# Hybrid S5 / sparse-attention layer: bias products, splits, sums and last scalings placed elsewhere in the program

## The chip, the cores and the metric

The kernel runs on one core of one Trainium2 chip. The metric is the device time of one execution in microseconds; of several runs the median is given. The engines are PE (TensorE: matmuls and transposes), DVE (VectorE), ACT (ScalarE), POOL (GpSimd) and SP (SyncE, which here only issues DMAs; ACT issues some too).

## What is computed (the reference)

One decoder layer on x of 1024 x 1024 float32 (one sequence, 1024 tokens, model width 1024):

```python
h = rmsnorm(x, norm_attn_g)
[u | q | k_cmp v_cmp k_slc v_slc k_win v_win | gates | g_a g_b] = h @ W_in
y_a = up_a(glu(s5(u)))                 # S5: 32 groups of 16 channels, state 64
y_b = up_b(nsa(q, k/v per branch, gates, T5 bias))   # 8 heads, 2 kv heads, head size 64
x  += (sigmoid(g_a) * y_a + sigmoid(g_b) * y_b) @ W_out
x  += (silu(n @ W_gate) * (n @ W_up)) @ W_down,  n = rmsnorm(x)   # inner width 2816
out = rmsnorm(x)
```

## The kernel before, in words

All float32 products are made of three: each operand is split into a high part (`wh`, `shi`, `mhi`: a cast on ACT or POOL) and a low part (`wl`, `slo`, `mlo`: a subtraction on DVE), and PE does high x high, low x high, high x low. A weight unit goes through three stages: SP loads it (`wr`), one engine casts it, DVE subtracts. `W.ahead(s, n)` keeps `s` units split and `n` loaded ahead of the next use.

The program runs in stages, and each engine takes its instructions in the order in which the code is written.

- *Projection with S5 beside it* (to some 370 us). The projection's matmuls (L414 to L416, called projection matmuls here) are interleaved with a side program, one step of it for so many matmuls. The side program makes the S5 in eight batches `b`: `tables(b)` (seven POOL operations L850 to L856, then `sn`, `xt`, `cs` on ACT), ways in and out (DVE, POOL), then per batch transposes, the kernel `kz`, eight transfers `tz<-kz` on SP, and `c<-ut,tz` products. `bias()` made eight pairs of matmuls (32x384 results, L824), each followed by a copy `brs` on ACT and a DMA on ACT, as eight steps ahead of the first batch. DMAs of SP and ACT share eight counters in turn, and one waits for the one before it on its counter. Then come `compress` and `glu` (whose `z` is split in eight pieces).
- *Attention*, then `up_b`, the merge: the output projection (`units`, L1491 to L1493) for 8 token tiles tt in the order (0, 1, 4, 5), (0, 4), (1, 5), (2, 3, 6, 7), (2, 3), (6, 7); the add to x (L1497), squares (L1504), roots, `norm` (L1511), and the transposes (`turned` for tt < 4; `turn`: sums and three further matrices T0, T1, T2 for tt >= 4).
- *Feed-forward, up*: a Strassen-Winograd scheme with seven products per matrix and 22 matrices (`rest`). Beside each, `self.chain` carries the sums (ch) of an earlier matrix through: loads of `sd`, two pairs of additions on DVE, stores to `ss`.
- *Feed-forward, down* (`down`): seven products p in the order 1, 5, 6, 3, 7, 2, 4, each over f = 0 to 10 (`order`, 77 steps). Step n splits step n+2's operands (`sr` from `sd` or `ss`, a weight block), loads step n+4's, and makes 12 matmuls (four token tiles of three). `beside` hangs other work on a step: chain sums, loads of x1, adds of the products to x1, squares and the last scalings. The last three steps go token tile by token tile, with `finish` for tiles 4 to 7.

Of the kernel before, what the change touches and what calls it, by code (L numbers as in the profile page):

```python
# [16 lines left out]
P = 128  # L17
# [19 lines left out]
NEAR = 6  # L37
# [86 lines left out]
class Winograd:  # L124
# [200 lines left out]
    def rest(self, n, early):  # L325
# [21 lines left out]
        next(self.chain, None)  # L347
# [6 lines left out]
        GP.tensor_tensor(p5, u3, p5, op=OP.add)  # L354
# [9 lines left out]
        self.t2(n + 1)  # L364
        if not early:
# [21 lines left out]
class Kernel:  # L387
# [83 lines left out]
    def transposed(self, tags, xs, hi, lo, tt):  # L471

        nc = self.nc
        for h in range(2):
# [7 lines left out]
            nc.vector.tensor_tensor(lo[:, o[0], o[1]], v, hi[:, o[0], o[1]], op=OP.subtract)  # L482

# [334 lines left out]
    def bias(self, pool):  # L818

        nc = self.nc  # L820
        for h in range(8):
            b = self.bank("c")
            for i in range(2):
                nc.tensor.matmul(b[:, 0:384], self.rbb[i][:, h, :], self.ohr, start=i == 0, stop=i == 1)  # L824
            s = pool.tile([P, 384], F32, name="brs", tag="brs", bufs=2)
            nc.scalar.copy(s, b[:, 0:384])
            nc.scalar.dma_start(self.bd[h], s)
            yield
# [30 lines left out]
    def s5(self):  # L859
# [64 lines left out]
        yield from self.bias(self.bs)  # L924
        zb = None
        for b in range(NB):
# [56 lines left out]
            AC.activation(f(zb[:, h]), q, AF.Gelu_apprx_tanh)  # L983
            yield
# [8 lines left out]
    def compress(self, pool):  # L993
# [27 lines left out]
        for _ in range(6):  # L1021
# [58 lines left out]
    def glu(self, pool):  # L1080
        nc, V = self.nc, self.nc.vector
        parts = []
        for h in range(2):
            parts.append([pool.tile([P, 4, 512], FR, name=n, tag=n, bufs=2) for n in ("zh", "zl")])
            for k in range(4):
                self.split(*(x[:, k, :] for x in parts[h]), self.z[h][:, k, :], "act", "dve")
                yield
# [343 lines left out]
    def up_b(self, pool, m_):  # L1431
# [28 lines left out]
        for n in range(4):  # L1460
            w = self.W.next("w_up_nsa", 0, 4, 256 * n, 256, ("act", "dve"))
            ps = [(i, h, self.bank("a")) for i in range(2) for h in range(2)]
            for kk in range(0, 4, 2) if n == 0 else (None,):
                for i, h, b in ps:
# [5 lines left out]
                    if kk != 0:  # L1470
                        merged(b, 2 * n + i, h)

    def merge(self, pool, m, td, xd, ffn):
# [4 lines left out]
        x1, xns, sq, tmp, ps = {}, {}, {}, {}, {}  # L1478
# [46 lines left out]
        def turn(what, tt, tags="bc"):  # L1525

            at, c = slice(P * tt, P * tt + P), slice(P * (tt - 4), P * (tt - 4) + P)
            first = lambda i, j: m[i][:, 4 * j:4 * j + 4, c].bitcast(F32)
# [7 lines left out]
            if what == "sums":  # L1536
# [4 lines left out]
                V.tensor_tensor(t1, pb, first(0, 0), op=OP.subtract)  # L1541
                V.tensor_tensor(t1, t1, first(1, 0), op=OP.subtract)
# [12 lines left out]
            elif what == "T4":  # L1555
                V.tensor_tensor(t3, first(0, 1), t1, op=OP.subtract)
                V.tensor_tensor(t3, t3, first(1, 1), op=OP.add)
# [3 lines left out]
        def turned(tt):  # L1561
            self.transposed("bc", xns.pop(tt), m[0], m[1], tt)

        def units(tts, q, between):

            banks = [self.bank("a") for _ in tts]
            for u in range(4):
                w = unit(u, q)
                for i, tt in enumerate(tts):
# [5 lines left out]
                    if u == 3:  # L1575
                        add(tt, q, banks[i])
                        if q and tt < 6:
# [3 lines left out]
                for f, *a in between.get(u, ()):  # L1581
# [9 lines left out]
        units((1, 5), 1, {(0, "m"): [(norm, 0), (root, 4)], 0: [(norm, 4)],  # L1591
                          2: [(turned, 0)] + T(4, "transpose", "sums"), (3, "m"): T(4, "T1", "B22")})
        units((2, 3, 6, 7), 0, {(0, "m"): T(4, "T3") + [(norm, 1), (root, 5)] + T(4, "T2"),
                                0: [(norm, 5)] + T(4, "T4"), (1, "m"): [(load, 2), (load, 3)],
# [27 lines left out]
    def down(self, pool, sd, ss, xd):  # L1622
# [39 lines left out]
        def combine(n):  # L1662
            while len(rb) < min(n, len(order)):
# [3 lines left out]
                if p in (5, 6, 7, 4):  # L1667
# [27 lines left out]
        sums = {}  # L1695

        def square(x, ss):
            scr = dn.tile([P, D], F32, name="scr", tag="scr", bufs=1)
            AC.activation(scr[:, 0:512] if x.shape[1] == 512 else scr, x, AF.Square, accum_out=ss)

        def scaled(tt, c, r, eng):
            x = x1[tt][:, c]
            self.scaled(x, x, r, gf[:, c], eng)
            nc.sync.dma_start(self.out[P * tt:P * tt + P, c], x)
# [19 lines left out]
        def beside(p, f):  # L1724

            if p == 4 and f < 4:
                V.tensor_tensor(half(4 + f, 1), half(4 + f, 1), gf[:, 512:D], op=OP.mult)
            if p == 1 and f < 8:
                if f % 4 == 0:
# [260 lines left out]
```

## Time and profile before

| | |
|---|---|
| median of 3 runs | 1602.8 us (1601.49 to 1607.31) |
| the profiled execution | 1604.1 us, span 1602.3 us, mean granted PE clock 0.984 |
| PE busy | 1528.9 us, 95% of the span, 7796 matmuls |
| DVE, ACT, POOL busy | 1015.7, 659.4, 642.0 us |
| HBM read, written | 153.61 MB, 59.37 MB (133 GB/s over the span) |

The first line says what is to be explained, the second that the profiled execution stands 1.3 us above the median. PE is the engine with the most work; the others have slack on average, though not in every stage. The page's slices show PE below 80% in two of 40 only.

### The profile page before, as it was taken

The page shows a single profiled execution, that of the slowest core. Times are in us where ns is not written, and L with a number is a line of the kernel's source. Part 1 is how long each engine was busy: PE and PEld are TensorE (multiplying, and loading weights), DVE is VectorE, ACT ScalarE, POOL GpSimd, SP SyncE. Part 2 cuts the span into 40 slices and gives each one's busy share as a digit, 9 for nine tenths or more (in the row PEclk, how much of TensorE's full clock was granted, in tenths as well). Part 3 has the DMA queues.
Part 4 walks back from the last instruction along what each step waited for, and adds up shares of the span by engine and source line. Part 5 has one row for each costly group of instructions (what it writes and reads, how often), then busy time and mean ns, then how long its engine had stood idle before and what let it go on. Part 6 is the DMA issues. An engine that isn't in the chain of part 4 may idle for free.

```text
span 1602.3 us, 22657 instructions
## 1 busy us (share of the span) xinstructions
PE 1528.9 (95%) x7796; PEld 1279.4 (80%) x7796; DVE 1015.7 (63%) x1916; ACT 659.4 (41%) x1354; POOL 642.0 (40%) x736
## 2 busy tenths in 40 slices
PE   8989999999999999999998989999999999799996
PEld 8867788888877899998777777888887877588884
DVE  7463786722335899998856665444456666486777
ACT  5221334411321698898126553333322223244444
POOL 1034767500012455555430128766777774000000
PEclk9999999999999999999999999999999999899998
DMA  7315343349247612100755522222235555875443
GB/s 222 107 63 168 112 139 98 81 117 266 84 151 231 184 30 66 43 28 16 223 181 168 197 79 79 79 86 86 79 112 182 194 177 204 285 234 173 128 133 125
DMA packets 184586, 216.59 MB, mean 135 GB/s; under 512 B 22810, under 2 KB 121526, under 8 KB 184471
## 3 DMA queue, kind: packets, MB, share of 16 engines
q1 hardware_dynamic: 175831, 199.93, 40.6%
q10 hardware_dynamic: 8640, 15.21, 2.6%
q8 instruction: 62, 1.02, 0.3%
q14 instruction: 53, 0.43, 0.1%
HBM read 153.61 MB, written 59.37 MB: 133 GB/s over the span
## 4 chain that ended last, share of the span: by engine, by line
PE 70%; DVE 10%; DMA 6%; ACT 5%; POOL 4%; issue 3%; SPq 1%; ACTq 0%; DVEq 0%; POOLq 0%
PE a L414 8%; PE a L416 7%; PE a L415 7%; PE O L1353 4%; PE a L220 4%; PE a L221 4%; PE a L222 4%; PE T L1335 3%; PE S L1237 3%; DVE wl L426 2%; DMA wr<-in_w_out 2%; ACT wh L423 2%; PE a L1721 2%; PE a L1722 2%; PE b L221 2%
## 5 line engine op out<-in xcount | busy, mean ns | idle before, releaser
L426 DVE TENSOR_TENSOR wl<-wr,wh 128x512 fp32r<-128x512 f32 (+1 forms) x142 | 160.0, 1139 | 140.8 <-ACT wh L423 96.1
L414 PE MATMUL a<-hhi,wh 128*128 128x512 f32 x448 | 183.5, 410 | 0.0
L416 PE MATMUL a<-hhi,wl 128*128 128x512 f32 x448 | 178.8, 399 | 1.5 <-DVE wl L426 1.5
L415 PE MATMUL a<-hlo,wh 128*128 128x512 f32 x448 | 178.5, 398 | 0.0
L1308 POOL TENSOR_SCALAR P<-P,sum,gates 128x640 f32<-128x640 f32 (+3 forms) x192 | 125.1, 667 | 115.6 <-DVE sum L1302 71.6
L220 PE MATMUL a<-mhi,wh 128*128 128x512 f32 (+1 forms) x360 | 139.1, 386 | 0.9 <-ACT p L235 0.3
L222 PE MATMUL a<-mhi,wl 128*128 128x512 f32 (+1 forms) x360 | 138.5, 385 | 1.0 <-DVE rstd L441 1.0
L221 PE MATMUL a<-mlo,wh 128*128 128x512 f32 (+1 forms) x360 | 138.4, 384 | 0.0
L423 ACT CAST wh<-wr 128x512 fp32r<-128x512 f32 (+1 forms) x110 | 78.0, 728 | 129.2 <-DMA wr<-in_w_out 40.9
L161 POOL TENSOR_SCALAR wr<-wr,gcol 128x256 f32<-128x256 f32 x176 | 94.3, 560 | 71.0 <-DMA wr<-in_w_ffn_up 68.1
L421 POOL TENSOR_SCALAR wh<-wr 128x1024 fp32r<-128x1024 f32 x32 | 33.7, 1052 | 205.6 <-PE a L415 116.6
L1337 DVE TENSOR_TENSOR PTl<-T,PTh 128x512 fp32r<-128x512 f32 (+3 forms) x200 | 104.2, 544 | 9.9 <-ACT PTh L1336 8.1
L414 PEld LDWEIGHTS a<-hhi,wh 128*128 128x128 f32 x448 | 85.4, 191 | 22.1 <-issue 4.1
L416 PEld LDWEIGHTS a<-hhi,wl 128*128 128x128 f32 x448 | 85.4, 191 | 22.1 <-DVE wl L426 1.9
L1288 ACT ACTIVATE P<-P,m 128x640 f32<-128x640 f32 (+7 forms) x128 | 95.8, 749 | 17.2 <-DVE m L1272 17.2
L415 PEld LDWEIGHTS a<-hlo,wh 128*128 128x128 f32 x448 | 85.6, 191 | 18.0
L423 ACT CAST shi<-sr 128x512 fp32r<-128x512 f32 x77 | 47.7, 620 | 122.5 <-issue 53.8
L1336 ACT CAST PTh<-T 128x512 fp32r<-128x512 f32 (+3 forms) x200 | 88.7, 476 | 20.8 <-PE T L1335 19.8
L426 DVE TENSOR_TENSOR wl<-S,wh 128x1024 fp32r<-128x1024 f32 x44 | 66.8, 1519 | 41.1 <-ACT wh L423 41.1
L1272 DVE CUSTOM_DVE_ANT_0 P<-S,B 128x640 f32<-128x640 f32 (+7 forms) x128 | 89.6, 700 | 2.8 <-PE T L1335 1.1
L1335 PE MATMUL T<-cst,P 128*128 128x128 f32 x592 | 87.2, 274 | 3.6 <-DVE PTl L1337 2.9
L426 DVE TENSOR_TENSOR slo<-sr,shi 128x512 fp32r<-128x512 f32 x77 | 54.5, 708 | 49.6 <-ACT shi L423 49.6
(445 smaller groups left out, 4069.6 us busy)
## 6 DMA issues: line engine op xcount, KB each, us to landing
wr<-in_w_in SPq DMA_DIRECT2D x28, 512.0 KB, 4.2
wr<-in_w_out SPq DMA_DIRECT2D x24, 512.0 KB, 5.1
wr<-in_w_ffn_gate SPq DMA_DIRECT2D x22, 512.0 KB, 4.0
wr<-in_w_ffn_up SPq DMA_DIRECT2D x22, 512.0 KB, 4.1
ch<-sd SPq DMA_DIRECT2D x44, 256.0 KB, 3.0
ss<-ch SPq DMA_DIRECT2D x44, 256.0 KB, 2.5
sr<-ss SPq DMA_DIRECT2D x44, 256.0 KB, 2.7
b<-in_w_ffn_down SPq DMA_DIRECT2D x38, 256.0 KB, 3.8
```

The lines of the kernel that those rows point to most:

```text
L220: mm(o, wh[:, k], bh[:, k, c], start=first and k == 0, stop=False, skip_group_check=True)
L221: mm(o, wh[:, k], bl[:, k, c], start=False, stop=False, skip_group_check=True)
L222: mm(o, wl[:, k], bh[:, k, c], start=False, stop=k == 3, skip_group_check=True)
L414: mm(ps, a, c, start=start and k == 0, stop=False, skip_group_check=True)
L415: mm(ps, a, d, start=False, stop=False, skip_group_check=True)
L416: mm(ps, b, c, start=False, stop=stop and k == nk - 1, skip_group_check=True)
L423: nc.scalar.copy(hi, src)
L426: (nc.gpsimd if lo_eng == "pool" else nc.vector).tensor_tensor(lo, src, hi, op=OP.subtract)
L1288: AC.activation(p[:, 0:nk], p[:, 0:nk], AF.Exp, bias=m[:, 0:1], scale=-1.0, accum_out=sm(0))
L1308: sc = lambda x, y, z: GP.tensor_scalar(x, x, a[:, y:y + 1], gate(z), op0=OP.mult, op1=OP.mult)
L1335: T.transpose(t[:, x, :], p[:, c:c + P], self.ident)
L1337: V.tensor_tensor(ol, t[:, 0:len(cc), :], oh, op=OP.subtract)
```

## The change

- `bias(pool, h)` makes one pair and is called once in each batch, after that batch's gelu; the side program has four empty steps where it had eight with a pair each.
- `compress` starts one step later; `glu` takes two steps per split instead of one.
- `up_b` calls `W.ahead(2, 4)` after its first row of the last unit.
- In `merge`, the squares and roots of tiles 4 and 5 and the T1/B22 splits come later; `turned` also copies the transposed banks to `raw` (two ACT copies per tile), and the sums subtract `raw` in one DVE operation where they subtracted high and low halves in two.
- In `rest`, the chain's step comes after `t2(n + 1)`; the last matrix's products and one add go from POOL to DVE.
- In `down`, the chains of the last two matrices move from (1, 0) to (1, 7) to other steps; sums of squares and the weight's `combine` are spread over earlier steps; the last scalings are done half by half, half 0 on DVE with its store on SP, half 1 on ACT with its store on ACT, with roots for 4, 2 and 2 tiles together.

```diff
@@ out(): last matrix
-            K.nc.gpsimd.tensor_tensor(t, t, self.gates.pop((j, i, h)), op=OP.mult)
+            eng = K.nc.vector if n + 1 == len(self.mats) else K.nc.gpsimd
+            eng.tensor_tensor(t, t, self.gates.pop((j, i, h)), op=OP.mult)
@@ rest()
         self.t1(n + 1)
-        next(self.chain, None)
...
         self.t2(n + 1)
+        next(self.chain, None)
@@ s5(), ahead of the batches, and in each
-        yield from self.bias(self.bs)
+        for _ in range(4):
+            yield
...
             AC.activation(f(zb[:, h]), q, AF.Gelu_apprx_tanh)
+            self.bias(self.bs, b)
             yield
@@ up_b()
+                    if n == 3 and i == 0 and h == 1:
+                        self.W.ahead(2, 4)
@@ merge(): sums, turned
-                V.tensor_tensor(t1, pb, first(0, 0), op=OP.subtract)
-                V.tensor_tensor(t1, t1, first(1, 0), op=OP.subtract)
+                V.tensor_tensor(t1, pb, first(0), op=OP.subtract)
...
-            self.transposed("bc", xns.pop(tt), m[0], m[1], tt)
+            x = raw[tt] = xns.pop(tt)
+            for h, ps in enumerate(self.transposed("bc", x, m[0], m[1], tt)):
+                AC.copy(x[:, 512 * h:512 * h + 512], ps)
...
-        units((1, 5), 1, {(0, "m"): [(norm, 0), (root, 4)], 0: [(norm, 4)],
-                          2: [(turned, 0)] + T(4, "transpose", "sums"), (3, "m"): T(4, "T1", "B22")})
+        units((1, 5), 1, {(0, "m"): [(root, 0), (norm, 0), (square, 4), (root, 4)], 1: [(norm, 4)],
+                          2: [(turned, 0)] + T(4, "transpose", "sums")})
@@ down(): beside
-            if p == 1 and f < 8:
-                if f % 4 == 0:
-                    sums["chain"] = self.chain(pool, sd, ss, NF - 2 + f // 4)
+            at = {(1, 3): 0, (1, 10): 1}.get((p, f))
+            if at is not None:
+                sums["chain"] = self.chain(pool, sd, ss, NF - 2 + at)
+            if (p, f) in ((1, 3), (1, 6), (1, 7), (1, 8), (1, 10), (5, 2), (5, 3), (5, 4)):
                 next(sums["chain"])
...
+        def finish(tt, r):
+            rows = slice(P * tt, P * tt + P)
+            V.scalar_tensor_tensor(half(tt, 0), half(tt, 0), r, gf[:, 0:512], op0=OP.mult, op1=OP.mult)
+            nc.sync.dma_start(self.out[rows, 0:512], half(tt, 0))
+            AC.activation(half(tt, 1), half(tt, 1), AF.Copy, scale=r)
+            nc.scalar.dma_start(self.out[rows, 512:D], half(tt, 1))
...
         split(len(order))
+        r = roots(0, 0, 4)
+        for tt in range(4):
+            finish(tt, r[:, tt:tt + 1])
```

Three places show what the change moves. The first is ACT at the start of the S5 batches: `sn`, `xt`, `cs` are the tables' values, `uv` and `evf` copies of projection results, `cd` a store, `brs` and `bd` the bias copies and their stores, `wt` the first batch's transposes. Before:

```order
L880 ACTIVATE sn<-xt 128x512
L881 ACTIVATE xt<-xt 128x512
L882 ACTIVATE cs<-xt,cst 128x512
L638 COPY uv<-a 128x64 x8
L624 COPY evf<-a 128x512
L625 DMA cd<-evf 128x512
L826 COPY brs<-c 128x384
L827 DMA bd<-brs 128x384
L826 COPY brs<-c 128x384
L827 DMA bd<-brs 128x384
```

and now:

```order
L641 COPY uv<-a 128x64 x8
L627 COPY evf<-a 128x512
L628 DMA cd<-evf 128x512
L627 COPY evf<-a 128x512
L628 DMA cd<-evf 128x512
L936 COPY wt<-b 128x512
L627 COPY evf<-a 128x512
L628 DMA cd<-evf 128x512
L880 ACTIVATE sn<-xt 128x512
L881 ACTIVATE xt<-xt 128x512
L882 ACTIVATE cs<-xt,cst 128x512
L627 COPY evf<-a 128x512
```

The bias copies and stores have left this place, and the second tables' values (the second `sn`, `xt`, `cs`) stand ahead of a fourth `evf` copy and its store.

The second is DVE at the start of the down projection: `slo`, `wl` are the low halves of the steps' operands (`wr`, `near`, `b`: the weight blocks), `ch` the chain's sums. Before:

```order
L426 TENSOR_TENSOR slo<-sr,shi 128x512
L426 TENSOR_TENSOR wl<-wr,wh 128x512
L1612 TENSOR_TENSOR ch<-ch 128x512
L1613 TENSOR_TENSOR ch<-ch 128x512
L426 TENSOR_TENSOR slo<-sr,shi 128x512
L426 TENSOR_TENSOR wl<-wr,wh 128x512
L1615 TENSOR_TENSOR ch<-ch 128x512
L1616 TENSOR_TENSOR ch<-ch 128x512
L426 TENSOR_TENSOR slo<-sr,shi 128x512
L426 TENSOR_TENSOR wl<-near,wh 128x512
```

and now:

```order
L427 TENSOR_TENSOR slo<-sr,shi 128x512
L427 TENSOR_TENSOR wl<-near,wh 128x512
L427 TENSOR_TENSOR slo<-sr,shi 128x512
L427 TENSOR_TENSOR wl<-b_13000,wh 128x512
L427 TENSOR_TENSOR slo<-sr,shi 128x512
L427 TENSOR_TENSOR wl<-b_13029,wh 128x512
L1617 TENSOR_TENSOR ch<-ch 128x512
L1618 TENSOR_TENSOR ch<-ch 128x512
L427 TENSOR_TENSOR slo<-sr,shi 128x512
L427 TENSOR_TENSOR wl<-b_13053,wh 128x512
```

The sums of the chain of the last matrix but one stood behind the low halves of the third step and in front of those of the fourth; now five more steps' halves go ahead of them.

The third is ACT at the end, behind the last split: `rstd` are the roots, `x1f` the scaled halves, `out` their stores. Before, all of it for tiles 4 to 7:

```order
L1699 ACTIVATE scr,ssf_14394<-x1f 128x512
L1699 ACTIVATE scr,ssf_14423<-x1f 128x512
L440 ACTIVATE rstd<-ssf_14851,eps 128x1
L1758 ACTIVATE x1f<-x1f,rstd 128x512
L1759 DMA out<-x1f 128x512
L1699 ACTIVATE scr,ssf_14452<-x1f 128x512
L440 ACTIVATE rstd<-ssf_14875,eps 128x1
L1758 ACTIVATE x1f<-x1f,rstd 128x512
```

and now:

```order
L441 ACT_TABLE_LOAD
L441 ACTIVATE rstd<-sq_14801,eps 128x4
L1764 ACTIVATE x1f<-x1f,rstd 128x512
L1765 DMA out<-x1f 128x512
L1764 ACTIVATE x1f<-x1f,rstd 128x512
L1765 DMA out<-x1f 128x512
L1764 ACTIVATE x1f<-x1f,rstd 128x512
L1765 DMA out<-x1f 128x512
L1764 ACTIVATE x1f<-x1f,rstd 128x512
L1765 DMA out<-x1f 128x512
L1703 ACTIVATE scr,ssf_12937<-x1f 128x512 x2
L441 ACTIVATE rstd<-sq_14850,eps 128x2
```

The square-root table's load and four scalings with their stores (tiles 0 to 3) now stand in front of the squares of tiles 4 and 5.

## Rows read from the trace of the kernel before

**Rows 1.** The page, part 1: busy us of each engine, share of the span, instructions.
```profile
PE 1528.9 (95%) x7796; PEld 1279.4 (80%) x7796; DVE 1015.7 (63%) x1916; ACT 659.4 (41%) x1354; POOL 642.0 (40%) x736
```

**Rows 2.** PE's waits in the whole span: us in total, times, longest.
```profile
PE a L1721 <- DVE wl L426: 13.9, 4, 9.8
PE c L824 <- ACT brs L826: 6.6, 1, 6.6
PE b L222 <- DVE wl L426: 3.5, 6, 0.8
PE a L1491 <- DVE x L1497: 3.4, 2, 3.2
PE c L220 <- ACT T2h L423: 3.1, 1, 3.1
...
PE a L1491 <- ACT wh L423: 2.1, 2, 1.2
PE c L1045 <- DMA w<-in_cmp_w_k: 2.1, 1, 2.1
```

**Rows 3.** PE's timeline, 120 to 127 us: start, us, engine, line, operation, [idle before].
```profile
120.92 0.68 PE L824 MATMUL c<-ohr,rbh 32*128 32x384 f32 x1 [6.62 <-ACT brs L826]
...
122.87 0.63 PE L416 MATMUL a<-hhi,wl 128*128 128x512 f32 x1
...
126.71 0.63 PE L416 MATMUL a<-hhi,wl 128*128 128x512 f32 x1
```

**Rows 4.** ACT's timeline, 111 to 112 us.
```profile
111.07 0.63 ACT L880 ACTIVATE sn<-xt 128x512 f32<-128x512 f32 x1 [14.45 <-POOL xt L856]
```

**Rows 5.** DVE's timeline, 116 to 119 us.
```profile
116.43 1.88 DVE L426 TENSOR_TENSOR wl<-wr,wh 128x1024 fp32r<-128x1024 f32 x1
```

**Rows 6.** POOL's timeline, 148 to 160 us: first and last of seven.
```profile
148.34 1.04 POOL L850 TENSOR_TENSOR ta<-cst,rh 128x512 f32<-128x512 f32 x1
...
158.65 0.62 POOL L856 TENSOR_SCALAR xt<-xt 128x512 f32<-128x512 f32 x1
```

**Rows 7.** SP's queue, 147 to 155 us.
```profile
147.46 7.05 SPq L947 DMA_DIRECT2D tz<-kz  x8
```

**Rows 8.** PE's timeline, 161 to 162 us.
```profile
161.49 0.38 PE L977 MATMUL c<-ut,tz 128*128 128x128 f32 x2
```

**Rows 9.** PE's timeline, 1375 to 1381 us: first and thirteenth start.
```profile
1375.41 0.79 PE L1721 MATMUL a<-wl,shi 128*128 128x512 f32 x1 [9.76 <-DVE wl L426]
...
1380.64 0.40 PE L1721 MATMUL a<-wl,shi 128*128 128x512 f32 x1
```

**Rows 10.** DVE's timeline, 1372 to 1374 us.
```profile
1372.73 0.69 DVE L1612 TENSOR_TENSOR ch<-ch 128x512 f32<-128x512 f32 x1 [10.19 <-DMA ch<-sd]
```

**Rows 11.** SP's queue, 1362 to 1369 us.
```profile
1362.39 2.01 SPq L1619 DMA_DIRECT2D ss<-ch  x4
1366.83 1.75 SPq L1609 DMA_DIRECT2D ch<-sd  x4
```

**Rows 12.** PE's timeline, 1576 to 1583 us.
```profile
1576.85 0.39 PE L1722 MATMUL a<-wh,slo 128*128 128x512 f32 x1
1577.08 0.39 PE L1720 MATMUL a<-wh,shi 128*128 128x512 f32 x1
...
1582.44 0.80 PE L1721 MATMUL a<-wl,shi 128*128 128x512 f32 x1 [2.50 <-DVE wl L426]
```

**Rows 13.** ACT's timeline, 1565 to 1599 us (ACTq: its DMA issues).
```profile
1565.30 1.28 ACT L440 ACT_TABLE_LOAD   x1
1566.59 0.29 ACT L440 ACTIVATE rstd<-ssf,eps 128x1 f32<-128x1 f32 x1
...
1596.79 0.29 ACT L440 ACTIVATE rstd<-ssf,eps 128x1 f32<-128x1 f32 x1 [0.45 <-DVE rstd L441]
1597.76 0.72 ACT L1758 ACTIVATE x1f<-x1f,rstd 128x512 f32<-128x512 f32 x1 [0.68 <-DVE rstd L448]
1598.51 0.37 ACTq L1759 DMA_DIRECT2D out<-x1f  x1
```

More of the change, by code (lines that the diff above doesn't have):

```diff
@@ L36 @@
 NPOW = 9
-NEAR = 6
+NEAR, EARLY = 6, 9
 def run(gen, n=None):
@@ L353, in rest @@
         V.tensor_tensor(u3, u2, v, op=OP.add)
-        GP.tensor_tensor(p5, u3, p5, op=OP.add)
+        (V if last else GP).tensor_tensor(p5, u3, p5, op=OP.add)
         if last:
@@ L816, in bias_parts, with bias @@
         self.split(*self.rbb, rbb, "act", "dve")
[L818 to L828, printed above, removed]
+    def bias(self, pool, h):
+        nc, b = self.nc, self.bank("c")
+        for i in range(2):
+            nc.tensor.matmul(b[:, 0:384], self.rbb[i][:, h, :], self.ohr, start=i == 0, stop=i == 1)
+        s = pool.tile([P, 384], F32, name="brs", tag="brs", bufs=2)
+        nc.scalar.copy(s, b[:, 0:384])
+        nc.scalar.dma_start(self.bd[h], s)
     def exp(self, out, x, pool, name, n):
@@ L1020, in compress @@
         ws = [w1(j) for j in range(4)]
-        for _ in range(6):
+        for _ in range(7):
             yield
@@ L1694, in down @@
         Vs = [self.bank("bbcc"[i]) for i in range(4)]
-        sums = {}
+        sums = {i: dn.tile([P, 8], F32, name=f"ssf{i}") for i in range(2)}
         def square(x, ss):
[L1698 to L1704, printed above, removed]
+            AC.activation(dn.tile([P, 512], F32, name="scr", tag="scr", bufs=1), x, AF.Square, accum_out=ss)
         def add(tt, c, ps):
@@ L1735, in beside @@
                     x1_loads(range(at[0], at[0] + 4), at[1])
+            if p == 2 and f >= 6:
+                for i in range(2 * f - 12, min(2 * f - 10, EARLY)):
+                    V.tensor_tensor(slot[0, i], slot[2, i], slot[0, i], op=OP.subtract)
             tt = f - 2
@@ L1742, in beside, with roots @@
             if 0 <= tt < 4:
+                if p == 7:
+                    square(half(tt, 1), sums[0][:, 4 + tt:5 + tt])
+                    V.tensor_tensor(half(tt, 1), half(tt, 1), gf[:, 512:D], op=OP.mult)
                 if p == 2:
[L1744 to L1745 removed]
+                    square(half(4 + tt, 1), sums[1][:, 4 + tt:5 + tt])
+                    V.tensor_tensor(half(4 + tt, 1), half(4 + tt, 1), gf[:, 512:D], op=OP.mult)
                 if p == 4:
[L1747 to L1760 removed]
+                    square(half(tt, 0), sums[0][:, tt:tt + 1])
+        def roots(i, a, b):
+            sq = dn.tile([P, b - a], F32, name=f"sq{b - a}", tag=f"sq{b - a}", bufs=2)
+            V.tensor_tensor(sq, sums[i][:, a:b], sums[i][:, 4 + a:4 + b], op=OP.add)
+            return self.rstd(dn, sq)
+        def finish(tt, r):
[4 more added lines that the diff above has]
+            nc.scalar.dma_start(self.out[rows, 512:D], half(tt, 1))
         last = len(order) - 3
@@ L1775, in down @@
                 products(n, tt)
-            if tt < 3:
-                beside(*order[last + tt])
             add(4 + tt, 0, U[tt])
-            square(half(4 + tt, 0), sums[4 + tt][:, 0:1])
-            if tt:
-                finish(tt - 1)
-        finish(3)
+            square(half(4 + tt, 0), sums[1][:, tt:tt + 1])
+            if tt == 1:
+                r = roots(1, 0, 2)
+                finish(4, r[:, 0:1])
+            if tt == 2:
+                finish(5, r[:, 1:2])
+        r = roots(1, 2, 4)
+        for tt in range(2):
+            finish(6 + tt, r[:, tt:tt + 1])
         dn.release()
```

40 lines of the change are left out of this document (13 added, 27 removed).

## The prediction, on record before the run

> **What bounds the kernel now.** The page's busy shares come first: TensorE (PE) works 1528.9 of 1602.3 us, 95% [rows 1], so only some 73 us of idle time, and the stretches at the lower granted clock, can be won without taking matmuls away. The change takes none away: the PE list has the same number of rows in both programs. So I read the view that sums PE's waits by line and releaser, for which wait costs most [rows 2]. Three kinds stand out: one place in the down projection (L1721 for wl: 13.9 us in four waits, one of 9.8), one in the bias products (L824: 6.6), and small ones of 1.5 to 3.5 in compress, merge and the Winograd stage. Then I went to each place in the timelines, to see what the releaser itself had waited for.
>
> **The pitch of a matmul.** Two starts in a row at full clock are 0.23 us apart [rows 12]. After the bias wait nine matmuls take 126.71 - 122.87 = 3.84 us, 0.43 each [rows 3]: the lower of the two clock levels. A long wait thus costs more than itself.
>
> **1. Bias products, spread over the batches.** Before, the third pair starts at 120.92 after 6.62 us of waiting for a copy on ACT [rows 3]. ACT was in `sn<-xt`, before which ACT had idled 14.45 us for POOL's tables [rows 4]. The move takes this wait away and 9 x (0.43 - 0.23) = 1.8 us of low clock with it. But what is late next stands close: the matmuls behind it need a weight's low half, whose subtraction DVE starts at 116.43 and ends at 118.3 [rows 5]. PE, without the two pairs that ran before, would be there at about 113, and waits about 5 us again. Further on, the first S5 batch now comes 39 projection matmuls sooner. It needs `tz`, eight transfers that SP issued from 147.46 [rows 7]. In the changed program those stand, on the counter that they share with ACT's transfers, behind an ACT store that comes after `sn`, `xt`, `cs` of the second tables. POOL takes from 148.34 to 159.27 for these [rows 6]. If their start moves up with the weight unit ahead of them to about 128, they end at 137 to 139; the ACT work, the store and the eight transfers put `tz` at 147.5 to 151 (an estimate, middle 149.3). PE arrives at 143.5 to 147, so a new wait of 0 to 7 us. The same progress: before, `c<-ut,tz` starts at 161.49 [rows 8] with eight bias pairs and 39 matmuls more done; after, 149.3 + 39 x 0.23 + 8 pairs x 0.46 (two pitches each, an estimate) = 162.0, and the new waits bring the low clock back, another 1.8: 163.8. Term: **-2** (a loss of 2), from -6 to +4. The wait that goes is alone worth 6.6 + 1.8 = 8.4; `tz` takes it back. The copies (and their stores) beside the later batches stand under 39 matmuls per batch: nothing.
>
> **2. Compress and glu.** Compress starts one step later, about nine matmuls = 2.1 us, and PE's wait there for `w` is 2.1 [rows 2]: gain 0 to 2.1. Glu gets its splits two steps apart; DVE's low halves meet the weight's own there. I take **+1.5** for both (-1 to +3, a slip of four DVE pieces of 0.7 to one missed).
>
> **3. Splits ahead of the merge.** PE's first matmuls of the output projection wait for wh (two waits, 2.1 in all [rows 2]), then for its low half. ahead(2, 4) puts both on ACT and DVE some dozen matmuls sooner, before the square-root table load. **+2** (0 to +3: the wh wait in full and a us of low clock above, nothing if the weight's transfer is what is late).
>
> **4. Merge.** PE waits 3.2 us once for the add `x` (3.4 in two [rows 2]). On DVE the add stands behind a run of subtractions. Three of these, a T1 sum and two low halves, now stand behind it: 3 x 0.6 (0.69 each [rows 10], less the overlap of two in a row) = 1.8. The wait for T2h is 3.1 [rows 2]; the chain to it loses two DVE pieces a tile, of which I count the last tile's 1.2. Against it stand eight more copies on ACT, two a tile. They lie beside weight casts that PE waits for, and a copy of this size in front of a cast makes it up to 0.7 late (0.72 with a scale [rows 13]). 1.8 + 1.2 = **+3**; -2 (seven of the eight in front of a cast that PE waits for, 5, less the 3) to +6 (both waits gone).
>
> **5. The Winograd matrices.** One chain step is moved a sum later, and the last matrix's products go from POOL to DVE. Waits of the kind L222 for wl are 3.5 us in six [rows 2]; one or two may go. DVE takes three more pieces of 0.69 once. **+1** (-1 to +3).
>
> **6. Into the down projection.** The long wait is the clearest. DVE stands at `ch`, the chain of matrix 20, from its last low half to 1372.73, 10.19 us [rows 10], for a load that SP could only issue at 1366.83, after the store at 1362.39 [rows 11]. The low half that PE needs, ready to be made, is queued behind it, so PE waits 9.76 to 1375.41, then runs at the low clock: 12 matmuls to 1380.64 in 5.23 us [rows 9] where 12 x 0.23 = 2.8 would do, 2.4 lost. Together 12.2. The change moves this chain's load to (1,3), its sums to (1,6) and (1,7), three steps of 12 matmuls (2.8 us each) later than the load. So the low half is made where it is ready. What is late next: the SP queue. The same store and load still stand on it in order, and SP issues no operand load in the 4.4 us between [rows 11]. With loads four steps ahead (11 us), that gap and the chain's four transfers beside them, I take off one step's worth, 3: **+9** (4 to 13, the upper end with a smaller wait of the same line just before it).
>
> **7. The end.** The last token groups start at 1577.08, and PE waits 2.50 us at 1582.44 for a low half [rows 12]; on DVE the splits stood among wide scalings. Now the sums and combines are spread before, so 36 matmuls x 0.23 = 8.3 and up to a us of waiting end PE 9.2 after the start (call it 0). But the roots of tiles 0 to 3 and their scalings now stand behind the last split, on DVE and ACT, in front of the last tiles. ACT: the root is ready at about 4.0 with the table load of 1.28 in it (two splits of DVE before it, an estimate); four times a copy of 0.72 and an issue of 0.37, to 8.6 with hand-overs; two squares at the price of the copy to 10; a root (from 1596.34, where ACT began to wait for it, to the copy at 1597.76: 1.4) to 11.4; copy and issue 12.5; square and finish 14.4, square 15.1, root 16.5, two finishes to 18.8; and 3.8 from the last issue to the span's end (1602.3 - 1598.5) [rows 13]: 22.6. Before: 1602.3 - 1577.08 = 25.2. **+2.6** (1 to 5; a split of both halves over ACT and DVE helps only while ACT is not the longer).
>
> The table load has a rule of its own. Rows: the load starts at 1565.30, takes 1.28, and the root starts at 1566.59 [rows 13], 1.29 later. The Trainium skill, "ScalarE: Activation LUTs", section "What ACT_TABLE_LOAD costs", gives about 1.28 us for the load and about 1.38 more for a drain, 2.66 together. Here, where the load now lies on the end's path, the sum by it would be 1.4 less, 15.7; the trace shows no such drain, so the sum goes by the row.
>
> **The sum.** -2 + 1.5 + 2 + 3 + 1 + 9 + 2.6 = 17.1 us. The profiled execution took 1604.1 (a span of 1602.3 and 1.8 around it), 1.3 over the median; 1604.1 - 17.1 = 1587.0, and against the median 1585.7. I predict **1586 us**, 1.0% faster.
>
> **Rivals.**
> A. The forecast: 1580 to 1591. The large term is a wait whose cause (one load ahead of splits in a queue) is in plain sight. Chance 0.60.
> B. The transition wait only moves: SP's loads, behind the store's 4.4 us, come late for the first steps, and 9 turns to 3. Sum 11, 1592. For it: SP issued no operand load for more than a step there [rows 11]. Against it: sr is four steps ahead. 0.16.
> C. Nothing much: transition 3, the bias term -4 (`tz` at 151), and ACT's copies eat the merge's gain (0). Sum -4 + 1.5 + 2 + 0 + 1 + 3 + 2.6 = 6: 1597, within 0.5% (8 us, about what can be told from no change). 0.17.
> D. Slower: the batches, 39 matmuls earlier, each wait for POOL's tables. A table takes 10.9 us [rows 6]. If each of eight batches stood 4 us for it, that is 32 in place of the 2 I took: 1603 - 19 + 32 = 1616. It decides from (19 + 8)/8 = 3.4 us a batch. Against it: only the first batch comes sooner against its tables; all later ones keep their distance in the matmul list. 0.07.
>
> So faster by over 0.5% is 0.76 (A, B), no difference 0.17, slower 0.07. The range is 1576 to 1598: A with the bias products and the transition at their good ends (+6 and +4 more), B, and most of C.
>
> **What the trace will show.** Right: no wait of the L1721 line (renumbered) over 3 us between 1355 and 1385; DVE's `ch` sums beside splits with no 10 us idle; the last store issued within 19 us of the last groups' start; a wait near 113 to 118 and one for `tz` in the place of the bias wait. Wrong: a wait of 5 us or more for `sr` in the first ten steps of the down projection (B); waits for `tz` or the tables in most batches (D); ACT ahead of a cast in the merge (C).

## The result, and the profile after

The changed kernel takes 1595.5 us (median of 5 runs, 1592.2 to 1597.1) against 1604.0 for the kernel before in the same session (5 runs, 1601.5 to 1607.3): the ratio is 0.994, with a 95% interval of 0.9918 to 0.9962. It is faster by 8.5 us, within the range on record, but the gain is half of the 17.1 us forecast. The profiled execution has a span of 1595.3 us, 7.0 below the 1602.3 of before. PE's busy time is the same to 0.1% [rows 1].

The page after, part 1, busy us by engine:

```profile
PE 1527.5 (96%) x7796; PEld 1282.1 (80%) x7796; DVE 1003.0 (63%) x1898; ACT 664.8 (42%) x1368; POOL 639.6 (40%) x732
```

To see where the time went I took the start times of matmuls that both programs have, and compared the stretches between them. The stretches, in us of the two profiled executions (gain positive):

| stretch of PE | before | after | gain | forecast |
|---|---|---|---|---|
| start of the program to the first projection matmul | 48.5 | 49.8 | -1.3 | 0 |
| to the first attention score (terms 1, 2) | 461.5 | 466.1 | -4.6 | -0.5 |
| to the last attention product | 248.3 | 248.0 | +0.2 | 0 |
| up_b, then output projection to the first Winograd product (terms 3, 4) | 166.0 | 167.1 | -1.1 | +5 |
| Winograd matrices, to the down projection (term 5) | 431.4 | 430.8 | +0.6 | +1 |
| first 11 steps of the down projection (term 6) | 45.0 | 34.1 | +10.9 | +9 |
| next 55 steps | 154.0 | 154.8 | -0.8 | 0 |
| last product to the span's end (term 7) | 47.8 | 44.7 | +3.1 | +2.6 |

The gains sum to 7.0, the difference of the spans. The last part of the program won what was forecast and a little more; the first half lost what was to be won there.

PE's waits in the whole span after, the costliest lines (us in total, times, longest), against [rows 2]:

```profile
PE c L978 <- DMA tz<-kz: 8.1, 1, 8.1
PE a L220 <- ACT p L235: 6.3, 5, 1.5
PE a L1496 <- DVE x L1502: 5.6, 3, 2.3
PE a L415 <- POOL m L906: 4.6, 1, 4.6
...
PE c L1047 <- DMA w<-in_cmp_w_k: 1.9, 1, 1.9
...
PE a L1720 <- DVE wl L427: 1.7, 2, 1.4
```

The 13.9 us in the down projection are down to 1.7, and the bias wait of 6.6 is gone. In their place stand three waits that were not on the list before (`tz`, ACT's `p`, POOL's `m`), and the waits for x have grown from 3.4 to 5.6. The first and the fourth line are the S5's start. PE's timeline after, 118 to 153 us, answering to [rows 3, 8]:

```profile
118.37 0.54 PE L415 MATMUL a<-hhi,wh 128*128 128x512 f32 x1 [4.59 <-POOL m L906]
...
152.59 0.77 PE L978 MATMUL c<-ut,tz 128*128 128x128 f32 x2 [8.08 <-DMA tz<-kz]
```

The first of these rows names POOL's `m`, which this matmul does not read; what it does need is its bank, which the copies `uv` empty, four on DVE and then four on ACT. In time order on DVE and ACT:

```profile
115.59 1.52 DVE L896 TENSOR_TENSOR w<-m,m 128x512 f32<-128x512 f32 x1 [0.95 <-POOL m L895]
117.03 0.60 DVE L641 COPY uv<-a 128x64 f32<-128x64 f32 x4
```

```profile
117.71 0.56 ACT L641 COPY uv<-a 128x64 f32<-128x64 f32 x4 [3.46 <-DVE uv L641]
```

ACT's copies end at 118.27, and PE starts 0.1 us later; POOL's `m` ended within that 0.1, so that the row names it. The copies stood on DVE behind the S5's `w`, whose first half had idled 9.83 us (at 113.23) for POOL's products behind the first tables.

What `tz` waited for is in the same stretch on POOL, ACT and SP (answering to [rows 6, 7]); the second tables end on POOL, ACT computes `sn` at once, and some 2.6 us later ACT's store is issued and SP's transfers after it:

```profile
129.66 1.04 POOL L850 TENSOR_TENSOR ta<-cst,rh 128x512 f32<-128x512 f32 x1
...
140.18 0.94 POOL L856 TENSOR_SCALAR xt<-xt 128x512 f32<-128x512 f32 x1
```

```profile
141.15 0.63 ACT L880 ACTIVATE sn<-xt 128x512 f32<-128x512 f32 x1 [13.62 <-POOL xt L856]
...
143.71 0.33 ACTq L628 DMA_DIRECT2D cd<-evf  x1
```

```profile
145.78 5.24 SPq L948 DMA_DIRECT2D tz<-kz  x8
```

POOL needs 11.5 us for these tables (141.12 - 129.66), SP issues the eight transfers from 145.78 to 151.02, and PE's product starts at 152.59. It was there at 144.5 (152.59 - 8.08).

At the down projection's start the picture is as forecast. DVE no longer idles at the chain's sums: the low halves run ahead of them, and the sums start without a wait. DVE's timeline after, 1371 to 1384 us, answering to [rows 10]:

```profile
1371.29 0.68 DVE L427 TENSOR_TENSOR wl<-wr,wh 128x512 fp32r<-128x512 f32 x1
...
1383.12 0.68 DVE L1617 TENSOR_TENSOR ch<-ch 128x512 f32<-128x512 f32 x1
```

Last, the end, on ACT (answering to [rows 13]): the last tile's scaling and store are at 1590.66 and 1591.41. The last token groups began at 1572.96, so the last store is issued 18.5 us after that, where 18.8 was worked out.

```profile
1590.66 0.72 ACT L1764 ACTIVATE x1f<-x1f,rstd 128x512 f32<-128x512 f32 x1 [0.45 <-ACT x1f L1764]
1591.41 0.34 ACTq L1765 DMA_DIRECT2D out<-x1f  x1
```

### The profile page after: what moved, and what is told of

It is laid out like the page before. It is cut to its first block, busy times and chain, and to the rows that moved or that the text cites. A ratio compares the mean times of both kernels' runs of the same rounds, so it can differ in the third digit from the quotient of the medians.

```text
span 1595.3 us, 22671 instructions
## 1 busy us (share of the span) xinstructions
PE 1527.5 (96%) x7796; PEld 1282.1 (80%) x7796; DVE 1003.0 (63%) x1898; ACT 664.8 (42%) x1368; POOL 639.6 (40%) x732
## 4 chain that ended last, share of the span: by engine, by line
PE 73%; DVE 8%; DMA 6%; ACT 5%; POOL 4%; issue 3%; SPq 1%; ACTq 0%; DVEq 0%; POOLq 0%
PE a L415 7%; PE a L416 7%; PE a L417 7%; PE a L220 4%; PE O L1356 4%; PE a L221 4%; PE a L222 4%; PE T L1338 4%; PE S L1240 4%; PE a L1720 2%; PE a L1719 2%; PE a L1721 2%; ACT wh L424 2%; DVE wl L427 2%; PE b L220 2%
## 5 line engine op out<-in xcount | busy, mean ns | idle before, releaser
L427 DVE TENSOR_TENSOR wl<-S,wh 128x1024 fp32r<-128x1024 f32 x44 | 63.3, 1439 | 41.4 <-ACT wh L424 41.3
```

The source lines that it names most:

```text
L427: (nc.gpsimd if lo_eng == "pool" else nc.vector).tensor_tensor(lo, src, hi, op=OP.subtract)
```

## The experiments

Times are medians; the ratio is to the kernel before, measured beside it on the same chip (medians of 1603.3 to 1604.8), with its interval. Stretches are from one profiled execution of each kernel, as in the table above.

**Bias pairs back ahead of the first batch (1586.4 us, ratio 0.9891, 0.9868 to 0.9915).**

```diff
-        for _ in range(4):
+        for h in range(8):
+            self.bias(self.bs, h)
             yield
```

> The changed kernel with the eight bias pairs back ahead of the first S5 batch, one per step, all else changed. Theory (the first batch comes 39 projection matmuls too soon and waits 8.1 us for tz): that wait is gone, the old one of some 6.6 for the bias copy is back, and the stretch from the first projection matmul to the first attention score, 461.5 us before and 466.1 after the change, is 460 to 462; the time is 4 to 6 us below the changed kernel. Rival (the stretch is longer because of the compress and glu steps, not of the bias products): it stays near 466 and the time with it.

Measured: the wait for `tz` is gone, the one for the copy `brs` is back with 6.6 us, and the stretch to the first score is 454.0. The time is 9.1 us below the changed kernel, more than expected, and the stretch 12.1 us shorter: with the batches four steps later compress does not wait either (1.9 us in the changed kernel for the weight `w`, and none here), and 2.5 us are a low-clock stretch at 57 to 63 us that this execution did not have (last section). The theory holds, the rival does not. The stretch is also 7.5 us below that of before, where the pairs and the batches stand in the same places: 2.7 of this is the same low-clock stretch, so the compress and glu steps alone won 4 to 5 us.

**Eight empty steps (1581.1 us, 0.9855, 0.983 to 0.9879).** The bias pairs stay spread, and only the first batch goes back to its place.

```diff
-        for _ in range(4):
+        for _ in range(8):
             yield
```

> The changed kernel, bias pairs still one in each batch, but eight empty steps instead of four ahead of the first batch, so that this batch stands where it stood before. Theory (only its coming sooner costs): the wait of 8.1 us for tz falls below 2, the wait of 4.6 near 118 us stays, the stretch from first projection matmul to first score is 457 to 460, the time 6 to 9 us below the changed kernel. Rival (the order of tz behind the store on ACT costs, wherever the batch stands): a wait of 5 us or more for tz or for the matmul behind it stays, and the time is within 2 us of the changed kernel.

Measured: 14.4 us below the changed kernel, twice what was expected. PE's waits between 80 and 520 us in this kernel, whole list:

```profile
PE a L415 <- POOL m L906: 4.6, 1, 4.6
PE S L1240 <- DVE sga L1136: 1.2, 1, 1.2
PE b L954 <- DVE wt L936: 0.6, 1, 0.6
```

The wait for `tz` is zero, that for compress too; the stretch is 451.5. The difference to the changed kernel, 14.6, is the wait of 8.1 with the low clock behind it, the wait of 1.9 and the 2.5 of the low stretch at 57 to 63 us that this execution did not have. Against the pairs ahead of the first batch (454.0, also without that stretch) spreading them is worth 2.5 us and not the wait of 6.6 that it removes, because the wait of 4.6 comes in its place. (The stretch without its first hundred projection matmuls is 425.2 with the pairs ahead, 422.0 to 423.7 in the eight kernels with eight steps.) Putting the first batch four steps sooner is what cost it.

**Six empty steps (1591.4 us, one run).** The edit is that of the eight steps, with 6 for 8.

> Six empty steps ahead of the first batch, between the changed kernel's four (wait for tz 8.1 us) and eight (no such wait). Theory (tz lands at its own time, and each step puts 9.6 matmuls of 0.23, or 2.2 us, in front of the matmul that needs it): a wait for tz of 3 to 5 us. Rival (the transfer moves with the batch, through the bias copies or the counters): 0 to 1, or 7 and more.

PE's waits between 80 and 520 us, the first two of four:

```profile
PE a L415 <- POOL m L906: 4.4, 1, 4.4
PE c L978 <- DMA tz<-kz: 3.2, 1, 3.2
```

With four, six and eight steps the wait is 8.1, 3.2 and 0. Two steps take 4.9 off; 2 x 2.2 = 4.4 was worked out. The number came as the theory said, the mechanism did not: `tz` has no time of its own. SP's transfers with six steps, then with eight, and the end of the second tables with eight:

```profile
136.26 13.98 SPq L948 DMA_DIRECT2D tz<-kz  x8
```

```profile
139.15 5.25 SPq L948 DMA_DIRECT2D tz<-kz  x8
```

```profile
147.63 0.61 POOL L856 TENSOR_SCALAR xt<-xt 128x512 f32<-128x512 f32 x1
```

With four steps the eight issues end at 151.02, behind the second tables. With six they begin before these tables end and run to 150.24, with two gaps in which ACT's stores `qd` (issued at 140.78 and 146.36, behind projection matmuls) land. With eight they are done at 144.40, before the tables end. What the transfers wait for is the ACT store that is ahead of them on a shared counter, and which store that is changes with the step. So the eight steps remove the wait twice over: PE comes at 150.55 in place of 144.5, and the last issue ends 6.6 us sooner.

**The merge as before, all else changed (1595.8 us, 0.9939, 0.9924 to 0.9955).** The functions of the merge were put back whole; up_b's early splits stay.

```diff
-                        if q and tt < 4:
+                        if q and tt < 6:
...
-        def turned(tt):
-            x = raw[tt] = xns.pop(tt)
-            for h, ps in enumerate(self.transposed("bc", x, m[0], m[1], tt)):
-                AC.copy(x[:, 512 * h:512 * h + 512], ps)
+        def turned(tt):
+            self.transposed("bc", xns.pop(tt), m[0], m[1], tt)
```

> The changed kernel with the merge as it was before (squares, roots, sums in two subtractions, no kept copies); the early splits of up_b stay. Theory (the weights' supply sets the pace of the merge, so its reorder only renames the waits): the stretch from the first low-half matmul of the output projection to the first Winograd product, 115.6 us before and 115.9 after the change, stays at 115 to 117, the time within 2 us. Rival (the reorder won its 3 us and the early splits lost as much): the stretch grows to 118 to 120.

Measured: the time is that of the changed kernel, and from the output projection to the down projection 547.1 us against 546.7 (114.5 and 432.6, against 115.9 and 430.8). The part is worth nothing that can be seen. PE's waits from 800 to 1000 us:

```profile
PE a L1496 <- DVE x L1502: 3.4, 2, 2.1
PE c L220 <- ACT T2h L424: 3.1, 1, 3.1
```

The T2h wait is 3.1 again, 1.7 with the change: that half of the step was right. But the waits for x are 3.4 here and 5.6 with the change, so what was won behind the merge was lost in it. In the kernels with the changed merge this stretch is 113.7 to 116.9 (nine profiles, the two edits of the merge below left out), so differences of 1 to 2 us in it tell nothing by themselves.

**The gate matrix's loads later (1583.8 us, 0.9876, 0.9858 to 0.9893), on the kernel of eight empty steps.**

```diff
-                                (1, "m"): [(ffn.load, 0)], 3: [(ffn.sums, 0)]})
+                                })
...
-"T1", "B22"), 2: T(5, "T3")})
-        units((2, 3), 1, {0: T(5, "T2"), 1: T(5, "T4")})
+"T1", "B22"), 2: T(5, "T3") + [(ffn.load, 0)]})
+        units((2, 3), 1, {0: T(5, "T2"), 1: T(5, "T4"), 3: [(ffn.sums, 0)]})
```

> Kernel of eight empty steps, with the two 512 KB loads of the first feed-forward matrix moved from the second weight unit of the output projection to two passes later. Theory (the loads of w_out, two at a time, set the pace of the merge, and these two loads stand between them on SP): the first wait of the merge for x (1.4 us) goes, the weight casts' waits for a landing fall by 3 us or more, and the stretch from the output projection to the first Winograd product, 116.9 us with eight steps, falls to 112 to 115. Rival (the chain of add, square, root, scale and transpose sets the pace): the stretch stays within 1 us of 116.9, and another wait takes the place of the first.

Measured: 117.2 us for the stretch, against 116.9. From 800 us on ACT's waits for a landing of the weights do fall, to 19.0 us (23.1 with eight steps), PE's for x do not (5.3 against 5.1), and a wait of 2.3 for a low half is new. My theory fell and the rival came: the loads that stood between are not what holds the merge.

**The adds first (1574.9 us, 0.9813, 0.9791 to 0.9836).** On the version put together (below), the add to x of a pass's last unit is issued ahead of the split of a later unit.

```diff
+                    if u == 3:
+                        add(tt, q, banks[i])
                     if i == 0:
                         self.W.ahead(2, 4)
...
                     if u == 3:
-                        add(tt, q, banks[i])
```

> The version put together, with one more edit in the merge: in a pass's last unit the add to x is issued ahead of the split of a later weight unit, not behind it. Theory (what the merge's products wait for is a PSUM bank that an add has not freed, and the add stands on DVE behind a low half whose weight has not landed): the waits for x, three of 1.3 to 2.3, fall to 2 us or less in all, and the stretch from the output projection to the first Winograd product, 115.2 us in the version put together, falls to 111 to 113.5. Rival (the weights or the chain of square, root and scale end the next wait anyway): the stretch stays within 1 us, with as much waiting for low halves or for xn.

In the changed kernel DVE has, from 836.7 to 840 us (answering to the add in [rows 2]):

```profile
836.70 1.23 DVE L427 TENSOR_TENSOR wl<-wr,wh 128x1024 fp32r<-128x1024 f32 x1 [6.13 <-ACT wh L424]
837.84 2.47 DVE L1502 TENSOR_TENSOR x<-x,a 128x512 f32<-128x512 f32 x4
```

and PE waits to 838.66 for the bank that the first of those adds frees. The adds stand behind a low half that has waited 6.1 us for its weight, which PE needs only two units later. At the other two waits for x a low half stands directly ahead of the add as well, but it has waited little or nothing; there DVE is simply busy. At the third (PE at 893.46):

```profile
891.50 1.22 DVE L427 TENSOR_TENSOR wl<-wr,wh 128x1024 fp32r<-128x1024 f32 x1
892.64 1.27 DVE L1502 TENSOR_TENSOR x<-x,a 128x512 f32<-128x512 f32 x2
```

With the adds first, PE's wait for x from 785 to 960 us is:

```profile
PE a L1495 <- DVE x L1501: 1.1, 2, 0.7
```

against, in the version put together:

```profile
PE a L1495 <- DVE x L1501: 4.9, 3, 2.3
```

The waits for x fall from 4.9 to 1.1, the stretch from 115.2 to 113.3. The theory holds for the wait: the bank that an add has not freed, because the add is queued behind a split, holds the products (that the split's weight had not landed is so at the first only). Some 2 of the 4 us come back as other waits, for low halves among them (2.0, before 1.2). The 1.9 us of the stretch are less sure: with the same merge the kernel of the matrices as before has 113.7.

**Winograd matrices as before (1578.3 us, 0.9843, 0.9828 to 0.9857), on eight steps.**

```diff
         self.t1(n + 1)
+        next(self.chain, None)
...
         self.t2(n + 1)
-        next(self.chain, None)
```

and the last matrix's products and one add again on POOL.

> Kernel of eight empty steps, with the Winograd matrices as before: the chain's step ahead of u3's sum, the last matrix's products and add on POOL. Theory (this part wins nothing that the end sees): the stretch from the first Winograd product through the first eleven steps of the down projection, 463.0 us with eight steps, stays within 1.5, the time within 2. Rival (the moved chain step is worth the 1 to 3 us forecast): the stretch is 1.5 to 3 longer, with waits of products for a low half of the weights in place of those for p.

Measured: 459.7 us against 463.0, and the time 2.8 lower. Both theories were wrong: the part costs about 3 us. The times alone would not show it (their intervals overlap), the stretch does: among the kernels with the changed merge and the moved down chains it is 462.9 to 466.3 in six with this part, 459.7 to 463.1 in four without. PE's waits from 1200 to 1345 us, with the change (eight steps) and then without this part:

```profile
PE a L220 <- ACT p L235: 5.9, 4, 1.5
PE b L222 <- DVE wl L427: 0.3, 1, 0.3
```

```profile
PE b L222 <- DVE wl L426: 1.5, 3, 0.8
PE b L220 <- ACT wh L423: 0.7, 1, 0.7
```

The chain's second pair of sums is behind t2 now, in front of u's sum on DVE, which is 1.3 us later for it:

```profile
1208.62 0.68 DVE L1620 TENSOR_TENSOR ch<-ch 128x512 f32<-128x512 f32 x1
1209.33 0.77 DVE L1621 TENSOR_TENSOR ch<-ch 128x512 f32<-128x512 f32 x1
1210.02 0.68 DVE L369 TENSOR_TENSOR u<-u,c 128x512 f32<-128x512 f32 x1
```

ACT, in order, waits with the gate of u, then a cast, then the copy p that frees PE's bank: 1.5 us at each of four matrices in this window. The old waits (for low halves) were smaller. The products on DVE were undone in the same run; they are in the last matrix only, and these waits are not.

**The changed down projection alone (1589.6 us, 0.991, 0.9886 to 0.9934).** `down` of the change in the kernel before.

```diff
-NEAR = 6
+NEAR, EARLY = 6, 9
```

and the function `down` as changed.

> The kernel before with the changed down projection alone (moved chains of the last two matrices, spread sums and combines, scalings on two engines). Theory (all that the change won is here): first matmul of the down projection to the span's end falls from 246.8 us by 12 to 14, and the time is 11 to 14 us below before. Rival (the chain step moved in the Winograd matrices and the products on DVE are needed for it, as the store of the last chain comes otherwise too late): the fall is under 8, with a wait of 3 us or more left in the first ten steps.

Measured: from the first down matmul to the span's end 246.8 before, 232.3 now, 14.5 less; the time is 14 below before, more than with the whole change. It needs no other part.

**Chains back (1590.5 us, one run), on the kernel with eight steps and the matrices as before.**

```diff
-            at = {(1, 3): 0, (1, 10): 1}.get((p, f))
+            at = {(1, 0): 0, (1, 4): 1}.get((p, f))
...
-            if (p, f) in ((1, 3), (1, 6), (1, 7), (1, 8), (1, 10), (5, 2), (5, 3), (5, 4)):
+            if (p, f) in [(1, i) for i in range(8)]:
```

> The kernel with eight empty steps and the matrices as before, with the chains of the last two matrices back on the steps (1,0) to (1,7) of the down projection. Theory (the long wait there is DVE standing at the chain's sums for their load): DVE idles 9 us or more at the sums, PE waits 8 to 10 us for a low half, and the first eleven steps take 42 to 46 us in place of 31.8. Rival (the spread sums, or the kinder start of the stage, remove the wait too): under 36.

Measured: DVE idles ahead of the chain's sum, and PE waits, in the first of these rows (DVE's timeline), and the second (PE's waits from 1340 to 1400 us):

```profile
1363.34 0.69 DVE L1616 TENSOR_TENSOR ch<-ch 128x512 f32<-128x512 f32 x1 [10.05 <-DMA sr<-sd]
```

```profile
PE a L1719 <- DVE wl L426: 10.0, 2, 9.6
```

The first 11 steps take 44.0 us, 12.3 more than with the chains moved. Both chains were put back; the trace has one long idle for it, at one pair of sums that stands in DVE's queue for a transfer, and with the low clock behind it that is the cost.

**Combines back (1580.6 us, one run), same kernel.** The weight's differences for the last product stand again in that product's steps.

```diff
-                if p in (5, 6, 7) or p == 4 and f >= EARLY:
+                if p in (5, 6, 7, 4):
...
-            combine(n + 3 + f // 2 if p == 3 else n + 3)
+            combine(n + 3)
```

> The kernel with eight empty steps and the matrices as before, with the weight combines of the last product back where they were, one in each of its steps; later sums and scalings stay as changed. Theory (DVE was over its 2.8 us a step only through the roots and 1.28 us scalings, which are elsewhere now; a combine of 0.6 a step fits): from the last product's first matmul to the last matmul 31 to 31.8 us, as now. Rival (the combines are what held the splits): 33 or more.

Measured: 31.0 us from the last product's first matmul to the last matmul, 31.0 with them spread. A combine per step fits. Before, this piece took 36.6 us; what did not fit is among the roots, sums and wide scalings that the change moved, and no run parts these.

**The last stores on SP (1581.4 us, 0.986, 0.9843 to 0.9876), on eight steps.**

```diff
-            nc.scalar.dma_start(self.out[rows, 512:D], half(tt, 1))
+            nc.sync.dma_start(self.out[rows, 512:D], half(tt, 1))
```

> Kernel of eight empty steps, with the last stores of half 1 issued by SP instead of ACT. Theory (ACT's own chain of copies, squares and store issues ends the program): eight issues of 0.37 leave ACT, of which four stand before the squares and four between the last roots and copies; from the last matmul to the span's end, 13.4 us, falls by 1 to 2.5, and the time by as much. Rival (the issue costs ACT no time that the end waits for, or SP's queue of sixteen stores is as late): within 0.5.

Measured: from the last matmul to the end 11.8 us, 13.4 with the stores on ACT, so the tail falls by 1.6 as expected. Between the two medians, 1581.4 and 1581.1, that does not show: the spread of each is 2.5 us or more.

**Together (1578.3 us, 0.9836, 0.9818 to 0.9855).** Eight empty steps, matrices as before, stores on SP.

> The version that the runs so far point to: the change with eight empty steps ahead of the first batch, the Winograd matrices as before, and the last stores of both halves on SP. Theory (the three are in different stages and add up): 1.6 us below the kernel with the matrices as before, 1576 to 1578, 1.6 to 1.8% below before; from the last matmul to the end 11.8 instead of 13.5. Rival (SP's queue of sixteen stores, or a lower clock elsewhere, takes it back): 1578 or more.

Measured: the tail is 11.8 again; the median is that of the kernel without the stores on SP, at the edge between theory and rival. The stores' part is below what this comparison tells. With the adds first (above) the ratio is 0.9813, 1574.9 us, the lowest median of the study (its interval overlaps with those of the last two kernels), 28 us below before and some 20 below the change as it was made.

## Why the prediction was right, and where it was not

**Bounding view.** Right: with PE's work unchanged, the sum of the waits decided, and nearly all of the gain is in the one long wait.

**1. Bias products.** The links to `tz` were right (tables on POOL, the store on ACT, the transfers behind it), and the size was not: PE waits 8.1 us, where 0 to 7 was said, as the tables took 11.5 us and started at 129.7, and PE came at 144.5. The new wait near 118 came with 4.6 where 5 was said, but for another reason: the matmul that waits reads no low half; it waits for its bank, and the low half is ready only 1.1 us later, for the third matmul. The stretch with terms 1 and 2 is 4.6 us longer (-0.5 forecast), and this sum hides two misses that offset each other. Undone by itself (the pairs ahead again) term 1 gives back 12.1 us, 2.5 of them the low-clock stretch, so as made it is nearer to -10 than to the -6 of its lower end. The forecast blamed the batch's coming sooner, rightly; eight, six and four steps show that without it the spread is a gain.

**2. Compress and glu.** Alone, beside the pairs ahead, it won 4 to 5 us, above the upper end of 3. In the changed kernel the wait in glu (1.5) is gone. The one in compress (1.9 against 2.1) is not, as S5 itself ended four steps sooner; with eight steps it is gone too.

**3 and 4. Up_b and merge.** Here the sum failed: forecast +5, measured -1.1. What was to go did go. The early splits remove the first waits for wh and its low half; T2h's wait falls by 1.4 where 1.2 was counted; and the wait for x that the forecast read, 3.2 us behind a run of subtractions, is 1.4, less by the 1.8 that was counted. What the sum left out is what came instead. At the first adds PE waits 1.9 (0.2 before), behind the low half that waits for its weight. The pieces moved behind one add stand ahead of a later one, where PE now waits 2.3. And ACT's last two copies stand ahead of a cast that PE waits for, the sign named for rival C:

```profile
921.02 0.59 ACT L1567 COPY xn<-c 128x512 f32<-128x512 f32 x1
921.51 1.66 ACT L424 CAST wh<-wr 128x512 fp32r<-128x512 f32 x3
```

```profile
922.18 0.50 PE L220 MATMUL a<-mhi,wh 128*128 128x512 f32 x1 [1.49 <-ACT wh L424]
```

With the merge as before PE has no such wait there (of the nine profiles with the copies, three have a longer wait for xn in its place). In sum PE's waits of 0.2 us and more from the output projection to the first Winograd product are 10.6 us before and 10.4 after: renamed, not removed. The adds put first take most of the waits for x away.

**5. Winograd.** Forecast +1. Against the kernel before, +0.6; but the same part undone gains 3.3 on that stretch and the next. The removed waits for low halves were bought with waits for p of 1.5. What went the other way in the stretch is T2h's 1.4, which falls into it, and low-clock stretches, which differ from execution to execution.

**6. Down projection's start.** Right: +10.9 against +9, from 4 to 13. The two waits left there, 1.1 and 1.4, are the residue; 3 were allowed. With the matrices as before (31.8 us) it gains two more. Rival B did not happen.

**7. The end.** Right: +3.1 against +2.6. The chain on ACT came out within 0.4 us of its sum. The table load stands in it; in the changed program too the root follows it at once (1.28 us load, root 1.29 us after its start):

```profile
1574.41 1.28 ACT L441 ACT_TABLE_LOAD   x1
1575.70 0.30 ACT L441 ACTIVATE rstd<-sq,eps 128x4 f32<-128x4 f32 x1
```

So the drain of the Trainium skill ("ScalarE: Activation LUTs", "What ACT_TABLE_LOAD costs") does not show here either, and the sum by the row was the right one.

**Rivals.** C's bias part came (worse than its -4), and the merge gave nothing, as in it, in part by the copies that it named; its small transition did not. The time stayed in the range because the two large terms at the end, 6 and 7, came out; the terms of the first half did not, and their errors in part cancelled, which is luck. D did not happen: one batch waited, not eight.

Left open: what ends the merge's remaining waits (xn, low halves, 5 us in all with the adds first), and whether the wait of 4.6 near 118 us goes with the `uv` copies ahead of the S5's `w` on DVE, which the rows suggest and no run here tried.

## What to carry to other kernels

An instruction that waits for a transfer holds everything behind it in its engine's queue: look for a pair of sums or a split in front of work that is ready, and move either; here that was the 10 us at the chain sums, and most of the 4.9 at the adds. When a wait is taken away in an interleaved program, ask what else comes sooner by it, and which transfers then stand behind which store: the same edit with four steps less of padding turned a gain into a loss. A piece moved behind one instruction stands ahead of another; look what waits for that one. Undo each part of a change alone: this one held a part worth +14 (the down projection), one worth -9 to -14 as placed (four steps) and one worth -3 (the moved chain step, undone together with the last matrix's products), and the sum hid them.

## What the runs showed of the hardware that was not expected

The low clock comes and goes between profiled executions at the same place, without a longer wait there. The fourteen kernels profiled here issue the same instructions in the first 84 us. Between 40 and 80 us the changed kernel (first row) and the one with eight steps (second) have:

```profile
40.00:80.00 40.00, 39.66 (x217) 34.18 (x216) 20.06 (x63) 9.47 (x25) 2.10 (x2) 0.91 0.36 107
```

```profile
40.00:80.00 40.00, 39.66 (x224) 34.19 (x223) 22.22 (x64) 9.41 (x25) 3.15 (x3) 1.00 0.36 107
```

The columns are the stretch, PE, weight loads, DVE, ACT and POOL busy, the granted clock, DMA share and GB/s. PE is as busy in both; the clock is 0.91 in one (0.52 from 57 to 63 us), full in the other, 11 more matmuls at 0.43 us and 2.5 us of time (from the first projection matmul to the one a hundred later 31.3 and 28.8 us). Over the fourteen kernels the granted clock of this window is 0.91 in six (the kernel before is one), 0.96 in six and 1.00 in two, and these hundred matmuls take 28.8 to 31.5 us. A stretch from one profiled execution is worth no more than that, and differences of 1 to 3 us between kernels here are read with it.
